# Moving SBUF tiles of a hybrid retention / gated-delta layer: weight buffers at a pitch of 2304 bytes instead of 2176, and everything behind the constants at multiples of 1024 bytes

## The chip, the cores and the metric

The kernel runs on one core of one Trainium2 chip. The metric is device time in microseconds: the median of the timed executions. One further execution was taken with the hardware profiler, and all rows below come from it.

## What is computed

One decoder layer on a float32 stream of 1024 tokens by 2048 columns. A conditioning vector gives shift, scale and gate; the scaled stream goes through one large projection; four retention heads and eight gated-delta heads work on its columns; an output projection, a gated residual and a LayerNorm end it. Cut to its core:

```
mod = silu(c) @ w_ada + b_ada; shift, scale, gate = split(mod, 3)
h = x * (1 + scale) + shift
[rq|rk|rv|rg|gqkv|gg|ga|gb] = h @ w_in              # 2048 x 7184
ret = groupnorm(retention(rotary(rq), rotary(rk), rv)) * silu(rg)
gdn = rmsnorm(gated_delta(l2norm(conv_silu(gqkv)), g(ga), sigmoid(gb))) * silu(gg)
y = concat(ret, gdn) @ w_out                        # 2048 x 2048
out = layernorm(2**0.25 * x + gate * y) * ln_w + ln_b
```

## The kernel before

**Split operands.** Each float32 operand of the two large projections is split into a high part (a cast to the type float32r, on ScalarE) and a low part (the rest, a subtraction, mostly on VectorE), and each product is three matmuls: high with high, high with low, low with high. The stream h stands transposed in SBUF as 16 pairs of tiles `h_hi`, `h_lo` of 128 x 1024 (4096 bytes of each partition). Weights come in units: SyncE's queue loads `w_raw`, L94 casts it to `w_hi`, L95 makes `w_lo`. Each of the three names has two buffers (`wp`, bufs=2), so units use the first and the second buffer in turn, each WU elements long.

**The three places with large matmuls.** `gemm_cm` (L410) makes a tile of 128 columns of the projection, transposed: the weights are stationary (128 x 128), h is the moving operand (512 columns). A unit has four row tiles, so 4 x 3 products x 2 halves = 24 matmuls; a tile has four units. `gemm_v` (L445) has h stationary and 256 weight columns moving, in units of 48 matmuls. The output projection (L1047) has pieces of the mixed heads (`ms`) stationary and 512 columns of the output weights (`wr`) moving; both live in row tiles of 4096 bytes.

**Order.** TensorE's order is written by hand: the projections call `tick()` after each matmul, and the heads' own steps are placed in between. The other engines' order, and that of SyncE's DMA queue, comes out of a scheduler that ranks instructions by what they wait for, a buffer's reuse included. TensorE's program starts with the conditioning (VectorE accumulates 16 row groups of `w_ada` into `acc`, L194), goes on with retention head 0, eight gated-delta heads, retention heads 1 to 3, and the output projection. The last gated-delta head's recurrence runs while `gemm_v` of retention head 1 is multiplied: per chunk VectorE makes `w` (L872) and the state `gs` (L887) from matmuls, and the next matmuls wait for them.

**Gate columns.** `gate_unit` (L372 to L392) loads 256 KB of `w_ada` into `graw` (one of the two buffers of the tag `gb`) and adds it to `gacc` on VectorE; 64 such units are called from the projections of retention heads 1 to 3, 16 of them in those of head 1. `gacc` and the second copy of the rotary table `rot` (1 MB, L482) stand in the pool `rp`, which is allocated on the right of SBUF when head 1 has its `gemm_v` behind it and the gated-delta pool `gp` on the left is given up.

**Where tiles stand.** Pools on the left grow up from byte 0 of each partition, those on the right down from the end. At 0 lies the descriptor scratch of the DMAs that GpSimd issues (16384 bytes by default), then the constants, then the tiles `h` and `ms`, then `w_raw`, `w_hi`, `w_lo` (later `raw`, `wr`), then the pools of the heads. In the program as built the `h` tiles start at 20960 and then every 4096 bytes; the two `w_hi` buffers at 156384 and 158560, the two `w_lo` buffers at 160736 and 162912; `gp` reaches up to 175824, and `rp`'s table is placed at 165600. A buffer of 544 elements is 2176 bytes, 8.5 times 256. So measured from a multiple of 256 bytes, all `h` tiles, `ms` and `wr` and the first buffers of `w_hi` and `w_lo` start 224 bytes behind it, the second buffers of both 96 bytes behind it. Steps inside a buffer are multiples of 512 bytes in `gemm_cm` and leave this as it is.

Of the kernel before, what the change touches and what calls it, by code (L numbers as in the profile page):

```python
# [7 lines left out]
F32 = mybir.dt.float32  # L8
# [7 lines left out]
P = 128  # L16
T = 1024
# [41 lines left out]
def hybrid_layer_kernel(ctx: ExitStack, tc: tile.TileContext, x, c, w_ada, b_ada, w_in, gdn_conv_w,  # L59
                        gdn_a_log, gdn_dt_bias, ret_gn_w, ret_gn_b, gdn_norm_w, w_out, ln_w, ln_b,  # L60
                        tab, out):
    nc = tc.nc
    V, S, G, PE = nc.vector, nc.scalar, nc.gpsimd, nc.tensor

    ctx.enter_context(tc.manual_schedule(engines={mybir.EngineType.PE}))
    const = ctx.enter_context(tc.tile_pool(name="const", bufs=1, side="left"))
# [15 lines left out]
    def load_const(name):  # L82
        lo, hi = TAB[name]
        t = const.tile([P, hi - lo], F32, name=name, tag=name)
        nc.sync.dma_start(out=t, in_=tab[:, lo:hi])
        return t

    WU = 544

    def split(raw, n, eng_l=None):  # L90
        hi = wp.tile([P, WU], F32R, name="w_hi", tag="w_hi")
# [26 lines left out]
            V.tensor_tensor(out=w, in0=w, in1=y, op=ALU.mult)  # L118
            V.scalar_tensor_tensor(out=y, in0=w, scalar=1.5, in1=y, op0=ALU.add, op1=ALU.mult)

# [1 line left out]
    ident = load_const("ident")  # L122
    cs = const.tile([P, KT], F32, name="cs")
    nc.sync.dma_start(out=cs, in_=c[0].rearrange("(p r) -> p r", r=KT))
    ones = const.tile([P, 1], F32, name="ones")
# [7 lines left out]
    cw = const.tile([P, 96], F32, name="cw")  # L133
    gnp = const.tile([P, 32], F32, name="gnp")

# [1 line left out]
    # The projections' sums over the first NA row tiles of g1, GDN k0 and v (two token tiles) wait in SBUF.  # L137
    NA = 5
    RATE = 1.7
    pa_ctx = ctx.enter_context(ExitStack())  # L140
# [4 lines left out]
    with ExitStack() as st:  # L145
# [75 lines left out]
                PE.transpose(ph[:, j * P:(j + 1) * P], xss[kt][:, 4 * i + j], ident)  # L221
            S.copy(xTs[kt][:, i * 512:(i + 1) * 512], ph)

        # The last item is the first unit of the next tile's weights.
        items = [(0, kt) for kt in range(NA)] + [(1, kt) for kt in range(KT)] + [(2, NA)]
        ps0 = []

# [105 lines left out]
    xid = load_const("xid")  # L333
    colsc, kdec, qdec = load_const("colsc"), load_const("kdec"), load_const("qdec")

    # Steps of the heads' own work wait here; the projections call tick() after each matmul, so that
    # each step is placed among matmuls that do not depend on it.
    # The heads' own sequence keeps its order; output steps (aux) come first when they are due.
    clock = [0.0]
    heads, aux, ao = [], [], [1]  # L340

# [24 lines left out]
    def small_ps():  # L366
        return ps.tile([P, 512], F32, name="ps", tag="ps")

# [1 line left out]
    gate_state = dict(i=0, acc=None)  # L370

    def gate_unit():  # L372
# [18 lines left out]
            V.tensor_tensor(out=row, in0=pgt[0:1, :], in1=row, op=ALU.add)  # L391
            nc.sync.dma_start(out=gate_d[:, cb * 512:(cb + 1) * 512], in_=row)  # L392

# [1 line left out]
    def gemm_cm(col, gate=False, part=None):  # L395
        pt = pg.tile([P, T], F32, name="pg", tag="pg")
        k0 = 0 if part is None else NA
# [77 lines left out]
                                       op0=ALU.add, op1=ALU.mult)  # L475
        return sg

# [1 line left out]
    def load_rot(pool, tag="rot"):  # L479
        lo, _ = TAB["rot"]  # L480
        t = pool.tile([P, 2, T], F32, name="rot", tag=tag)
# [115 lines left out]
            store(out=mixed[kti][:, tsl], in_=mx)  # L597
            yield 0

# [1 line left out]
    def conv_silu(pt, ti):  # L601
        y = mp.tile([P, T], F32, name="yc", tag="y", bufs=3)
        S.activation(out=y, in_=pt, func=AF.Copy, scale=cw[:, 72 + ti:73 + ti])  # L603
# [95 lines left out]
    def gdn_keys(h, st, k, dec, Pm):  # L699
        sup = mp.tile([P, 2048], F32, name="sup", tag="x8")  # L700
        A = sup[:, 0:1024].rearrange("p (j i) -> p j i", i=32)
        nb = c4(sup[:, 1024:2048])
        kt_ = mp.tile(B8, F32, name="ktok", tag="ktok")
        ss = gp.tile([P, NC], F32, name="ssk", tag="ssk")
        ets = []
        for hf in range(2):
            gb = gate_rows(h, hf)
            decay_matrix(h, hf, gb, gb, dec)
            ets.append(c4(gb))
        for hf in range(2):  # L710
            pk = small_ps()
            for j in range(4):
                ch = 4 * hf + j
                PE.transpose(pk[:, j * P:(j + 1) * P], k[:, ch * P:(ch + 1) * P], ident)
            sum_squares(pk, ss[:, 4 * hf:4 * hf + 4])
            V.tensor_tensor(out=kt_[:, 4 * hf:4 * hf + 4], in0=c4(pk),
                            in1=dec["ktl"][:, 4 * hf:4 * hf + 4, h:h + 1].broadcast_to(B4), op=ALU.mult)
            yield 4
        rk = gp.tile([P, NC], F32, name="rk", tag="rk")
        sk = gp.tile([P, NC], F32, name="sk", tag="sk")  # L720
        co = gp.tile([P, NC], F32, name="co", tag="co")
        nco = gp.tile([P, NC], F32, name="nco", tag="nco")
        V.tensor_scalar(out=ss, in0=ss, scalar1=1e-6, scalar2=None, op0=ALU.add)
        rsqrt(gp, rk, ss, NC, "k")
        V.tensor_tensor(out=sk, in0=ss, in1=rk, op=ALU.mult)
        V.tensor_tensor(out=rk, in0=rk, in1=rk, op=ALU.mult)
        V.tensor_tensor(out=co, in0=rk, in1=dec["beta"][:, :, h], op=ALU.mult)
        V.tensor_scalar(out=nco, in0=co, scalar1=-1.0, scalar2=None, op0=ALU.mult)
        for hf in range(2):
            pkk = small_ps()  # L730
            for j in range(4):
                cl = slice((4 * hf + j) * P, (4 * hf + j + 1) * P)
                PE.matmul(pkk[:, j * P:(j + 1) * P], k[:, cl], k[:, cl], start=True, stop=True)  # L733
            for j in range(4):
                ch = 4 * hf + j
                V.scalar_tensor_tensor(out=nb[:, ch], in0=pkk[:, j * P:(j + 1) * P], scalar=nco[:, ch:ch + 1],
                                       in1=ets[hf][:, j], op0=ALU.mult, op1=ALU.mult)
            yield 2
        # 32x32 diagonal blocks of the inverse: each partition has one block and eight of its rows
        s1 = drs.tile([4, NC, 1024], F32, name="s1", tag="s1")  # L740
        for b in range(4):
            bs = slice(32 * b, 32 * b + 32)
            nc.sync.dma_start(out=s1[b].rearrange("c (j i) -> j c i", i=32), in_=nb[bs, :, bs])
        for b in range(4):
            nc.sync.dma_start(out=A[32 * b:32 * b + 32].rearrange("p j i -> p (j i)"),
                              in_=s1[b][None].broadcast_to([4, NC, 1024]))
        X_ = gp.tile([P, 288], F32, name="X", tag="X")
        G.memset(X_, 0.0)
        G.tensor_copy(X_.rearrange("p (m i) -> p m i", i=36)[:, :, 0:4], xid[:, None, :].broadcast_to([P, 8, 4]))
        X = X_[:, :256].rearrange("p (m i) -> p m i", i=32)  # L750
        tmp = gp.tile([P, 8, 32], F32, name="xt", tag="xt")
        for j in range(31):
            cnt = j // 4 + 1
            if cnt <= 2:
                for m in range(cnt):
                    V.scalar_tensor_tensor(out=X[:, m, j + 1:], in0=A[:, j, j + 1:], scalar=X[:, m, j:j + 1],
                                           in1=X[:, m, j + 1:], op0=ALU.mult, op1=ALU.add)
            else:
                sh = [P, cnt, 31 - j]
                V.tensor_tensor(out=tmp[:, :cnt, j + 1:], in0=X[:, :cnt, j:j + 1].broadcast_to(sh),  # L760
                                in1=A[:, j:j + 1, j + 1:].broadcast_to(sh), op=ALU.mult)
                V.tensor_tensor(out=X[:, :cnt, j + 1:], in0=X[:, :cnt, j + 1:], in1=tmp[:, :cnt, j + 1:], op=ALU.add)
        s2 = drs.tile([4, 8, 4, NC, 32], F32, name="s2", tag="s2")
        for b in range(4):
            nc.sync.dma_start(out=s2[b].rearrange("m g c i -> (g c) m i"), in_=X[32 * b:32 * b + 32])
        for b in range(4):
            bs = slice(32 * b, 32 * b + 32)
            nc.sync.dma_start(out=Pm[bs, :, bs], in_=s2[b].rearrange("m g c i -> (m g) c i"))
        st.update(kt=kt_, nb=nb, sk=sk, co=co, due=clock[0] + BASE_WAIT)
# [149 lines left out]
        store(out=mixed[8 + h][:, hs], in_=mx)  # L919
        yield 0  # L920

# [1 line left out]
    gab = const.tile([P, NC, 16], F32, name="gab")  # L923
    with tc.high_priority():
        q_, k_ = (mp.tile([P, T], F32, name="qk0", tag=tag) for tag in ("ktok", "et"))
# [19 lines left out]
    for h in range(GH):  # L945
# [3 lines left out]
        v = conv_silu(gemm_cm(GV + h * P), 16 + h)  # L949
# [21 lines left out]
            if r < RH - 1 or e == 0:  # L971
                gate_ready(sgs, pt)
    ph1.close()
# [1 line left out]
    wp = ctx.enter_context(tc.tile_pool(name="wp2", bufs=1, side="left", reuse_waits="tile"))  # L975

    rings = dict(raw=0, wr=0)

    def ring(tag, n, m):
        """The first n of n + m tiles take the space that is free first."""  # L980
        i = rings[tag]
        rings[tag] = i + 1
        return dict(tag=tag, bufs=n) if i % (n + m) < n else dict(tag=tag + "_", bufs=m)

    def split_tile(src, own=False, urgent=True):
        """A row tile's high part and, beside it, the rest."""
        raw = wp.tile([P, 512], F32, name="raw", **ring("raw", 4, 2))
        with ExitStack() if own else tc.high_priority():
            nc.sync.dma_start(out=raw, in_=src)
        t = hp.tile([P, T], F32R, name="ms", tag="h") if own else wp.tile([P, T], F32R, name="wr", **ring("wr", 3, 1))  # L990
        with tc.high_priority() if urgent else ExitStack():
            S.copy(t[:, :512], raw)  # L992
        with tc.high_priority() if urgent else ExitStack():
            V.tensor_tensor(out=t[:, 512:], in0=raw, in1=t[:, :512].bitcast(F32), op=ALU.subtract)  # L994
        return t
# [27 lines left out]
    for hf in range(2):  # L1023
# [4 lines left out]
        for cb in range(4):  # L1028
# [92 lines left out]
            if not last:  # L1121
                rows = []
# [68 lines left out]
```

## Time and profile before

| what | us |
|---|---|
| timed executions (three) | 1993.68, 1992.58, 1999.07; median 1993.68 |
| span of the profiled execution | 2000.5, which is 6.8 over that median |
| TensorE busy in it | 1884.4 (94%) |
| VectorE, ScalarE, GpSimd busy | 1173.2, 552.2, 245.8 |
| TensorE's chain lines L410, L1047, L445 | 44%, 13%, 6% of the span |

A row of the page's groups reads: line, engine, operation, output<-inputs, shapes, count, then busy time, mean duration of one, and idle time of the engine just before. Matmuls overlap, so their pace is the distance from start to start, not the mean duration. Windows give busy time per engine in a stretch; PEclk is the share of TensorE's full clock that was granted.

### The profile page before, as it was taken

How to read it: one execution, taken by the hardware profiler on the slowest of the kernel's cores; microseconds unless marked ns; L12 is line 12 of the kernel's file. 1: busy time of each engine (PE TensorE's matmuls, PEld its weight loads, DVE VectorE, ACT ScalarE, POOL GpSimd, SP SyncE). 2: the span in 40 equal slices, each digit the busy share in tenths (PEclk: the TensorE clock that was granted, in tenths of full speed). 3: DMA queues.
4: the chain of work that ended last, by engine and by line, in shares of the span. 5: the costliest groups of instructions: out<-in, count | busy, mean ns of one | idle time of the engine just before them, and what ended most of it. 6: DMA issues, size and time to landing. Idle time of an engine off the chain costs nothing.

```text
span 2000.5 us, 27960 instructions
## 1 busy us (share of the span) xinstructions
PE 1884.4 (94%) x10272; PEld 1580.9 (79%) x10272; DVE 1173.2 (59%) x2943; ACT 552.2 (28%) x1241; POOL 245.8 (12%) x203
## 2 busy tenths in 40 slices
PE   3788999999999999999999999999999999998996
PEld 3566887787878888787878898898898878886885
DVE  7987346656675757475575744544542534459557
ACT  2433223232323232322323231211211232234221
POOL 3544001000000010000000010010010010005102
PEclk9899999999999999999999999999999999999998
DMA  9995322222221222222221224144141157345532
GB/s 269 277 282 151 83 65 71 59 67 59 66 57 46 72 52 72 48 69 56 70 57 46 72 80 126 43 143 132 41 134 48 44 187 249 110 145 173 191 108 96
DMA packets 293387, 210.76 MB, mean 105 GB/s; under 512 B 44969, under 2 KB 253050, under 8 KB 292482
## 3 DMA queue, kind: packets, MB, share of 16 engines
q1 hardware_dynamic: 290626, 200.59, 36.3%
q0 software_dynamic: 2624, 8.39, 1.2%
q8 instruction: 80, 1.31, 0.3%
q14 instruction: 57, 0.47, 0.1%
HBM read 190.01 MB, written 18.92 MB: 104 GB/s over the span
## 4 chain that ended last, share of the span: by engine, by line
PE 71%; DMA 5%; DVE 4%; issue 1%; ACT 1%; POOL 1%; SPq 0%; ACTq 0%; DVEq 0%; POOLq 0%
PE pg L410 44%; PE po L1047 13%; PE pg L445 6%; DMA gb<-gc_d 3%; DMA raw<-mixed 2%; DVE et L695 1%; PE ps L892 1%; PE ps L876 1%; PE ps L870 1%; PE ps L733 1%; PE ps L891 1%; PE ps L882 1%; PE ps L543 1%; DMA graw<-in_w_ada_dram 0%; DVE z L1102 0%
## 5 line engine op out<-in xcount | busy, mean ns | idle before, releaser
L410 PE MATMUL pg<-h_hi,w_hi 128*128 128x512 f32 x1420 | 470.2, 403 | 0.1
L410 PE MATMUL pg<-h_hi,w_lo 128*128 128x512 f32 x1420 | 466.2, 402 | 2.1 <-DVE w_lo L95 2.1
L410 PE MATMUL pg<-h_lo,w_hi 128*128 128x512 f32 x1420 | 465.0, 401 | 0.0
L94 ACT CAST w_hi<-w_raw 128x512 fp32r<-128x512 f32 (+3 forms) x239 | 146.5, 613 | 679.2 <-PE pg L410 481.9
L1047 PE MATMUL po<-wr,ms 128*128 128x512 f32 x1380 | 319.4, 392 | 11.2 <-DVE wr L994 7.9
L1047 PEld LDWEIGHTS po<-wr,ms 128*128 128x128 f32 x1380 | 259.3, 189 | 69.5 <-DVE wr L994 10.7
L410 PEld LDWEIGHTS pg<-h_hi,w_lo 128*128 128x128 f32 x1420 | 265.5, 189 | 55.4 <-DVE w_lo L95 3.3
L410 PEld LDWEIGHTS pg<-h_lo,w_hi 128*128 128x128 f32 x1420 | 266.5, 189 | 52.7
L410 PEld LDWEIGHTS pg<-h_hi,w_hi 128*128 128x128 f32 x1420 | 265.4, 189 | 53.7 <-ACT w_hi L94 1.7
L95 DVE TENSOR_TENSOR w_lo<-w_raw,w_hi 128x512 fp32r<-128x512 f32 (+2 forms) x217 | 153.9, 710 | 218.5 <-ACT w_hi L94 213.3
L994 DVE TENSOR_TENSOR wr<-raw,wr 128x512 fp32r<-128x512 f32 x116 | 88.0, 763 | 108.6 <-ACT wr L992 108.6
L445 PE MATMUL pg<-w_lo,h_hi 128*128 128x256 f32 (+1 forms) x502 | 143.4, 286 | 2.1 <-DVE w_lo L95 2.1
L445 PE MATMUL pg<-w_hi,h_hi 128*128 128x256 f32 (+1 forms) x502 | 143.5, 286 | 0.1
L445 PE MATMUL pg<-w_hi,h_lo 128*128 128x256 f32 (+1 forms) x502 | 143.3, 286 | 0.0
L992 ACT CAST wr<-raw 128x512 fp32r<-128x512 f32 x116 | 71.4, 621 | 155.6 <-PE po L1047 145.9
L194 DVE SCALAR_TENSOR_TENSOR acc<-wa,cs,acc 128x256 f32<-128x256 f32 x224 | 111.8, 564 | 4.0 <-DMA wa<-in_w_ada_dram 3.2
L445 PEld LDWEIGHTS pg<-w_lo,h_hi 128*128 128x128 f32 x502 | 95.1, 190 | 3.1 <-DVE w_lo L95 3.0
L445 PEld LDWEIGHTS pg<-w_hi,h_hi 128*128 128x128 f32 x502 | 95.2, 190 | 2.2 <-ACT w_hi L94 1.7
L445 PEld LDWEIGHTS pg<-w_hi,h_lo 128*128 128x128 f32 x502 | 95.1, 190 | 0.0
L606 DVE SCALAR_TENSOR_TENSOR yc<-pg,cw,yc 128x1023 f32<-128x1023 f32 (+2 forms) x69 | 88.2, 1279 | 2.9 <-ACT yc L603 2.0
L385 DVE SCALAR_TENSOR_TENSOR gacc<-graw,cs,gacc 128x512 f32<-128x512 f32 x60 | 48.4, 807 | 55.7 <-DMA graw<-in_w_ada_dram 55.3
L212 POOL TENSOR_TENSOR h_lo<-xT,h_hi 128x1024 fp32r<-128x1024 f32 x16 | 52.0, 3252 | 85.9 <-ACT h_hi L211 85.9
(243 smaller groups left out, 2235.7 us busy)
## 6 DMA issues: line engine op xcount, KB each, us to landing
w_raw<-in_w_in_dram SPq DMA_DIRECT2D x216, 256.0 KB
wa<-in_w_ada_dram SPq DMA_DIRECT2D x128, 256.0 KB
raw<-in_w_out_dram SPq DMA_DIRECT2D x128, 256.0 KB
graw<-in_w_ada_dram SPq DMA_DIRECT2D x64, 256.0 KB
xs<-in_x_dram SPq DMA_DIRECT2D x16, 512.0 KB
gb<-gc_d SPq DMA_DIRECT2D x32, 256.0 KB
raw<-mixed SPq DMA_DIRECT2D x32, 256.0 KB
z<-in_x_dram SPq DMA_DIRECT2D x32, 256.0 KB
```

What stands on the lines that cost most here:

```text
L94: S.copy(hi[:, :n], raw[:, :n])
L95: (eng_l or V).tensor_tensor(out=lo[:, :n], in0=raw[:, :n], in1=hi[:, :n].bitcast(F32), op=ALU.subtract)
L194: V.scalar_tensor_tensor(out=a, in0=wr, scalar=cs[:, r:r + 1], in1=a, op0=ALU.mult, op1=ALU.add)
L212: G.tensor_tensor(out=h_lo, in0=xT, in1=h_hi.bitcast(F32), op=ALU.subtract)
L385: V.scalar_tensor_tensor(out=a, in0=raw[:, :512], scalar=cs[:, r:r + 1], in1=a, op0=ALU.mult, op1=ALU.add)
L410: PE.matmul(pt[:, i * 512:(i + 1) * 512], w[:, kk], hh[:, i * 512:(i + 1) * 512], start=(kt == k0 and w is hi and hh is hH[kt]), stop=(kt ...
L445: PE.matmul(dst(tt), hh[:, tsl], w[:, kk], start=(kt == k0 and first_in_bank and hh is hH[kt] and w is hi), stop=(kt == KT - 1 and hh is h ...
L543: PE.matmul(po[:, :DV], sc[:, ch], vt[:, ch], start=(ch == 0), stop=True)
L606: V.scalar_tensor_tensor(out=y[:, s:], in0=pt[:, :T - s], scalar=cw[:, j * 24 + ti:j * 24 + ti + 1], in1=y[:, s:], op0=ALU.mult, op1=ALU.add)
L992: S.copy(t[:, :512], raw)
L994: V.tensor_tensor(out=t[:, 512:], in0=raw, in1=t[:, :512].bitcast(F32), op=ALU.subtract)
L1047: PE.matmul(pts[tt], m[:, a + tt * P:a + (tt + 1) * P], w, start=(n == 0 and a == 0 and w is wh), stop=(n == KT - 1 and a == 512))
```

## The change

Three numbers of placement: WU grows from 544 to 576 elements, so that a buffer is 2304 bytes, 9 times 256; a constant tile `pad` of 136 elements is put behind `ident`, with one column of it written; and the descriptor scratch is made 4096 bytes. No instruction's shape changes.

```diff
-    WU = 544
+    WU = 576
...
     ident = load_const("ident")
+    pad = const.tile([P, 136], F32, name="pad")
+    V.memset(pad[:, 0:1], 0.0)
     cs = const.tile([P, KT], F32, name="cs")
...
-    nc = _bacc.Bacc("TRN2", target_bir_lowering=False, num_devices=1)
+    nc = _bacc.Bacc("TRN2", target_bir_lowering=False, num_devices=1,
+                    dynamic_dma_scratch_size=4096)
```

Comments are dropped as well, and two lines come in ahead of the rest, so that a line of the kernel before stands two lines lower after. In the changed program the `h` tiles start at 9216 and then every 4096 bytes; the `w_hi` buffers at 144896 and 147200, the `w_lo` buffers at 149504 and 151808, all at multiples of 256; `raw`, `wr`, `ms` at multiples of 1024. The pools on the right, among them all tiles into which the conditioning and the inputs are loaded, stand where they stood. The left side is about 11 KB shorter: `gp` ends at 164848, below the table of `rp` at 165600.

So `rp` no longer shares bytes with `gp`, and the scheduler orders its tiles anew. TensorE's, ScalarE's and GpSimd's order is the same; SyncE's and VectorE's differ at these places. In SyncE's queue, at the start of the heads (before):

```order
L625 DMA alog<-in_gdn_a_log_dram 128x8
L482 DMA rot<-in_tab_dram 128x2048
L103 DMA w_raw<-in_w_in_dram 128x3x128
L626 DMA dtb<-in_gdn_dt_bias_dram 128x8
L103 DMA w_raw<-in_w_in_dram 128x4x128 x2
L103 DMA w_raw<-in_w_in_dram 128x3x128
```

and in the changed program:

```order
L627 DMA alog<-in_gdn_a_log_dram 128x8
L484 DMA rot<-in_tab_dram 128x2048
L103 DMA w_raw<-in_w_in_dram 128x3x128
L628 DMA dtb<-in_gdn_dt_bias_dram 128x8
L484 DMA rot<-in_tab_dram 128x2048
L103 DMA w_raw<-in_w_in_dram 128x4x128 x2
```

The second table load has moved here, some 1000 us ahead of its first use. In the same queue, in retention head 1 (the rows 2x256 are units of `gemm_v`, 4x128 those of `gemm_cm`), before:

```order
L678 DMA gb<-gc_d 128x4x128
L379 DMA graw<-in_w_ada_dram 128x512
L103 DMA w_raw<-in_w_in_dram 128x2x256
L379 DMA graw<-in_w_ada_dram 128x512
L103 DMA w_raw<-in_w_in_dram 128x2x256 x4
L482 DMA rot<-in_tab_dram 128x2048
L379 DMA graw<-in_w_ada_dram 128x512 x2
L103 DMA w_raw<-in_w_in_dram 128x4x128
L379 DMA graw<-in_w_ada_dram 128x512 x4
L103 DMA w_raw<-in_w_in_dram 128x4x128
```

and in the changed program:

```order
L680 DMA gb<-gc_d 128x4x128
L381 DMA graw<-in_w_ada_dram 128x512
L103 DMA w_raw<-in_w_in_dram 128x2x256
L381 DMA graw<-in_w_ada_dram 128x512 x6
L103 DMA w_raw<-in_w_in_dram 128x2x256
L381 DMA graw<-in_w_ada_dram 128x512 x4
L103 DMA w_raw<-in_w_in_dram 128x2x256
L381 DMA graw<-in_w_ada_dram 128x512 x5
L103 DMA w_raw<-in_w_in_dram 128x2x256
L381 DMA graw<-in_w_ada_dram 128x512 x2
L103 DMA w_raw<-in_w_in_dram 128x2x256
L103 DMA w_raw<-in_w_in_dram 128x4x128 x16
```

Sixteen further gate loads now stand between units of `gemm_v` instead of between those of `gemm_cm`. VectorE's order in the last gated-delta head's recurrence follows this; before:

```order
L885 COPY gs<-ps 128x128
L872 SCALAR_TENSOR_TENSOR w<-ps,neg,vs 128x128
L887 SCALAR_TENSOR_TENSOR gs<-gs,egl,ps 128x128
L872 SCALAR_TENSOR_TENSOR w<-ps,neg,vs 128x128
L95 TENSOR_TENSOR w_lo<-w_raw,w_hi 128x512
L887 SCALAR_TENSOR_TENSOR gs<-gs,egl,ps 128x128
```

and in the changed program:

```order
L384 TENSOR_SCALAR gacc<-graw,cs 128x512
L887 COPY gs<-ps 128x128
L874 SCALAR_TENSOR_TENSOR w<-ps,neg,vs 128x128
L387 SCALAR_TENSOR_TENSOR gacc<-graw,cs,gacc 128x512 x2
L889 SCALAR_TENSOR_TENSOR gs<-gs,egl,ps 128x128
L387 SCALAR_TENSOR_TENSOR gacc<-graw,cs,gacc 128x512
L874 SCALAR_TENSOR_TENSOR w<-ps,neg,vs 128x128
L387 SCALAR_TENSOR_TENSOR gacc<-graw,cs,gacc 128x512
L95 TENSOR_TENSOR w_lo<-w_raw,w_hi 128x512
L889 SCALAR_TENSOR_TENSOR gs<-gs,egl,ps 128x128
```

All 16 sums of the first gate block now stand among the recurrence's steps.

## Rows read from the trace of the kernel before

**Rows 1.** The page's head, and its line of busy times.

```profile
span 2000.5 us, 27960 instructions
PE 1884.4 (94%) x10272; PEld 1580.9 (79%) x10272; DVE 1173.2 (59%) x2943; ACT 552.2 (28%) x1241; POOL 245.8 (12%) x203
```

**Rows 2.** Windows: stretch, length, busy time (instructions) per engine, PEclk, DMA share, GB/s.

```profile
50.00:100.00 50.00, 36.05 (x166) 29.88 (x166) 48.73 (x91) 21.59 (x29) 26.80 (x12) 0.86 1.06 277
166.00:320.00 154.00, 142.19 (x802) 123.37 (x801) 83.78 (x201) 46.40 (x92) 21.77 (x20) 0.99 0.29 75
540.00:650.00 110.00, 107.69 (x626) 88.83 (x625) 69.61 (x217) 32.48 (x97) 7.96 (x9) 1.00 0.23 58
1180.00:1200.00 20.00, 20.00 (x173) 20.00 (x172) 7.30 (x23) 4.57 (x15) 1.61 (x2) 1.00 0.34 118
1200.00:1220.00 20.00, 20.00 (x150) 19.08 (x149) 10.74 (x15) 3.79 (x5) 0.58 (x1) 1.00 0.63 190
1318.00:1337.00 19.00, 18.57 (x156) 18.37 (x156) 10.74 (x14) 4.35 (x8) 3.79 (x4) 1.00 0.55 169
```

**Rows 3.** The page's groups: the large matmuls of the three places.

```profile
L410 PE MATMUL pg<-h_hi,w_hi 128*128 128x512 f32 x1420 | 470.2, 403 | 0.1
L410 PE MATMUL pg<-h_hi,w_lo 128*128 128x512 f32 x1420 | 466.2, 402 | 2.1 <-DVE w_lo L95 2.1
L410 PE MATMUL pg<-h_lo,w_hi 128*128 128x512 f32 x1420 | 465.0, 401 | 0.0
...
L1047 PE MATMUL po<-wr,ms 128*128 128x512 f32 x1380 | 319.4, 392 | 11.2 <-DVE wr L994 7.9
...
L445 PE MATMUL pg<-w_hi,h_hi 128*128 128x256 f32 (+1 forms) x502 | 143.5, 286 | 0.1
```

**Rows 4.** TensorE's timeline, retention head 1: every twelfth row of L410 (start, us, ...).

```profile
1214.98 0.62 PE L410 MATMUL pg<-h_hi,w_hi 128*128 128x512 f32 x2
...
1220.56 0.62 PE L410 MATMUL pg<-h_hi,w_hi 128*128 128x512 f32 x2
...
1226.03 0.64 PE L410 MATMUL pg<-h_hi,w_hi 128*128 128x512 f32 x2
...
1231.62 0.62 PE L410 MATMUL pg<-h_hi,w_hi 128*128 128x512 f32 x2
...
1237.08 0.64 PE L410 MATMUL pg<-h_hi,w_hi 128*128 128x512 f32 x2
```

**Rows 5.** The chain that ended last: start, us, matmuls without a gap.

```profile
869.23 23.05 PE pg L410 x100
...
1200.82 14.32 PE pg L445 x120
1215.14 48.84 PE pg L410 x212
...
1659.99 137.60 PE po L1047 x607
```

**Rows 6.** Timeline of the last gated-delta head's recurrence, TensorE and VectorE.

```profile
1163.76 0.35 DVE L872 SCALAR_TENSOR_TENSOR w<-ps,neg,vs 128x128 f32<-128x128 f32 x1 [0.97 <-PE ps L870]
...
1164.52 0.38 PE L876 MATMUL ps<-w,Pm 128*128 128x128 f32 x2
...
1166.12 0.35 DVE L887 SCALAR_TENSOR_TENSOR gs<-gs,egl,ps 128x128 f32<-128x128 f32 x1 [2.01 <-PE ps L882]
1167.73 0.35 DVE L872 SCALAR_TENSOR_TENSOR w<-ps,neg,vs 128x128 f32<-128x128 f32 x1 [1.27 <-PE ps L870]
```

**Rows 7.** VectorE's gate sums: their tile's group (ns), and its waits (us, times, longest).

```profile
L385 DVE SCALAR_TENSOR_TENSOR gacc<-graw,cs,gacc x60: 746/752/1762, 1195.9 to 1493.7; 128x512 f32<-128x512 f32 x60
...
DVE gacc L385 <- DMA graw<-in_w_ada_dram: 55.3, 46, 3.9
```

**Rows 8.** GpSimd's DMAs: packets, MB, share of 16 engines; median us to landing.

```profile
q0 software_dynamic: 2624, 8.39, 1.2%
...
mixed<-mxr POOLq DMA_DIRECT2D x12, 256.0 KB, 3.3
```

## The prediction

> **What bounds the kernel now.** I read the page's line of busy times first, then windows over the whole span, then TensorE's chain. TensorE is busy for 1884.4 of 2000.5 us [rows 1]. Until about 170 us it waits: in 50 to 100 us it is busy for 36 of 50 us while VectorE has 48.7 and the DMA engines are full [rows 2]. From there on it hardly stops: 107.7 of 110 us in a gated-delta head, 20.00 of 20.00 at 1180 and at 1200 us, at the full clock [rows 2]. So before 170 us TensorE's pace is worth nothing, and behind it nearly every nanosecond of a large matmul is a nanosecond of the kernel. The large matmuls are 3 x 1420 of L410, 1380 of L1047 and 3 x 502 of L445 [rows 3], 7146 together.
>
> **The pace of L410 has two values.** The reader should look at where units begin in a stretch where nothing is interleaved. Twelve rows of two matmuls are one unit of 24. The units take 1220.56 - 1214.98 = 5.58, then 5.47, 5.59 and 5.46 us [rows 4]: long and short in turn. Per matmul that is (5.58 + 5.59) / 48 = 232.7 ns and (5.47 + 5.46) / 48 = 227.7 ns. The two w buffers alternate with the units, and by the program's operand addresses the first and third of these units have their weights in the second buffers, 96 bytes behind a multiple of 256; the second and fourth have the first buffers, 224 bytes behind one, like the h tiles that stream past them. The mean over such stretches is the same elsewhere: 48.84 / 212 = 230.4 ns and, inside a gated-delta head, 23.05 / 100 = 230.5 ns [rows 5]; half of 232.7 and half of 227.7 is 230.2. The output projection, whose both operands stand at 224, runs at 137.60 / 607 = 226.7 ns [rows 5]. So weights that stand at another distance from a multiple of 256 than the moving operand cost about 5 ns, and weights at the same distance do not.
>
> A page speaks against this. The Trainium skill (SBUF — State Buffer, "Who interferes with whom") gives TensorE two independent read ports for the moving and the stationary operand and says that it never waits on anyone; by it a tile's place could not change the pace, and the change would be worth nothing in TensorE. The trace does not agree: 5.58 against 5.47 us for the same 24 matmuls [rows 4].
>
> **The change, part by part.**
>
> *Weights at multiples of 256.* After it both buffers and h have distance 0, so by the reading above all units run at the short pace. Half of 4260 matmuls, 2130, gain 5.0 ns each: 10.6 us. A matmul next to an interleaved step of a head is paced by that step too; I take off a little for these and count -10. From the same rows the least is 0 (something else than the distance alternates), the most is that L410 comes down to the 226.7 ns of the output projection, (230.4 - 226.7) x 4260 = 15.8 us.
>
> *L445 and L1047.* L445 runs at 14.32 / 120 = 119.3 ns for 256 columns [rows 5], a stretch that has both buffers in it; I see no second pace to remove and count 0, with 1 ns either way, 1.5 us, as bounds. L1047 has equal distances already: 0.
>
> *The common distance, 0 instead of 224.* No large matmul of the trace starts at a multiple of 256, so only bounds can be had. Below: 512 columns take 226.7 ns and 256 take 119.3, so a column takes 0.42 ns and each matmul has 226.7 - 214.8 = 11.9 ns on top. If all of that came from starting off a multiple, 7146 x 11.9 = 85 us would go. Above: all of L410 and L1047 at the slow 232.7 ns, which is 2.3 x 4260 + 6.0 x 1380 = 18 us more. The nearest rows are the two with equal distances (L410's short units and L1047, a nanosecond apart), so I take 0.
>
> *Gate sums among the last gated-delta head's recurrence.* 16 sums of 0.75 us [rows 7] now stand before `w` and `gs` on VectorE, and what is queued behind a sum that waits for its load is the recurrence, for which TensorE waits. VectorE is idle there for 1.27 us before `w` and for 2.01 us before `gs` [rows 6], so two sums per chunk of 4 us fit if their data is there. `w` is ready at 1164.11 and is used at 1164.52 [rows 6]: the slack is 0.4 us. A late load costs what exceeds it: in its stretches `gacc` waited for 55.3 / 46 = 1.2 us per load [rows 7]. At best nothing, at worst 16 x 1.2 = 19 us. Where the same sums and loads stand between units of `gemm_v` in head 2, TensorE lost 0.43 us of 19 [rows 2], but no gated-delta recurrence ran there. I take +2, nearer to that row. Where the sums stood before, TensorE was busy for all of 1200 to 1220 us [rows 2], so taking them away there gives nothing.
>
> *The second table load at the start of the heads.* 1 MB in a stretch where the DMA engines are busy for 0.29 [rows 2]; at the 277 GB/s of the full queue it takes 3.8 us, ahead of weight loads. The two weight buffers loaded ahead cover that: 0, and 3.8 us if they do not.
>
> *Scratch of 4 KB, pad.* GpSimd issues 36 stores, 2624 packets in all [rows 8], 73 per store and under 5 per engine, tens of microseconds apart: 0. If the last four waited for the one ahead, 4 x 3.3 = 13 us [rows 8], the bound. `pad` is one memset of one column at the start, where VectorE waits: 0. The tiles of the first 170 us that VectorE and the DMA fill on the right have not moved: 0.
>
> **Sum.** -10 + 2 = -8 us: 1992.5 on the profiled span of 2000.5. That span is 6.8 us over the median of the runs shown, so I put the same difference on the median: 1993.68 - 8 = 1986, with -14 to -2 around it, 1980 to 1992. A difference of under 0.3%, 6 us, is about what a measurement of this kernel cannot tell from no change.
>
> **Rivals.**
>
> *The on-top part shrinks too.* Speaking for it: two placements that differ only by 128 bytes already differ by 5 ns, so a start inside such a stretch may cost in itself. Against it: L410's short units and L1047 end at one value, and no row has a start at 0. A quarter of 11.9 ns is 21 us, half is 43, so with the -8 it gives 1965 to 1943, and at the very least 1901. The Trainium skill (TensorE: Matmul & The Clock Gate, "Wait — 56ns, not 53.3ns?") measures about 2.5 ns on top of a bf16 stream; as an estimate from that page, 9.4 x 7146 = 67 us would go. No run here shows it for this type.
>
> *The place does not matter.* If the alternation belongs to something else that comes with every second unit, or to the ports as the page has it, only the +2 remains: 1996, the same within 0.3%. Against it stand the equal tiles h on both sides of the alternation and the one constant pace of L1047.
>
> *Distance 0 is a bad one.* If what counts is not the equal distance but the place itself, 224 being good and 96 bad, then 0 may be as 96 is. All units of L410 are then at 232.7 ns and L1047 follows: 18 + 2 = 20 us more, 2014. It decides as soon as the common pace of L410 is above 230.4 ns. Nothing in the trace speaks for or against 0 itself.
>
> *The recurrence eats the gain.* With every sum late by its 1.2 us, -10 + 19 = +9, so 2003. It turns the sign from 0.6 us per sum on.
>
> **Chances.** My forecast 52%; the on-top part as well 17%; no effect of the place 17%; 0 a bad place 8%; the recurrence 6%. Of the forecast's share I put three fifths below -6 us: faster by over 0.3% is 0.31 + 0.17 = 0.48. Within 0.3%: 0.21 + 0.14 + 0.02 = 0.37. Slower: 0.03 + 0.08 + 0.04 = 0.15. The range leaves out the lower half of the on-top case and the bad place: 1950 to 2004; the forecast's own is 1980 to 1992.
>
> **What would show it.** Unit starts of L410 in head 1 at equal distances of 5.46 to 5.48 us, and a chain row of about 227.5 ns per matmul, show the first step right; 5.58 and 5.47 in turn show it wrong; all at 5.58 is the bad place. A pace of L1047 clearly under 226.7 ns is the on-top part. Waits of TensorE for `w` and `gs` between 1160 and 1195 us, and of `gacc` for `graw` on VectorE there, show the price of the gate sums; TensorE idle behind 185 us by 3 us more would be the table load. The prediction is wrong if the common distance 0 has a pace of its own, which no row could tell.

## The result

| | before | after |
|---|---|---|
| timed executions, same chip (six each) | 1992.58 to 1999.07 us, median 1996.5 | 1983.53 to 1989.22 us, median 1987.06 |
| ratio of after to before, 95% interval | | 0.9947 [0.9932, 0.9961] |
| span of the profiled execution | 2000.5 us | 1984.3 us |

The change makes the kernel faster by 0.53%, 9.4 us of 1996.5. The two profiled executions lie 16.2 us apart, which is more: each is one execution, executions of one kernel spread over 6 us here, and the profiled one of before is none of its six and longer than all of them. In a later set of executions, in which both kernels took longer, the pair stood at 0.9960 (below).

The profile after, read in the order of the rows of before. A line of the kernel before stands two lower. The page's head, busy times and groups of large matmuls, which answer to [rows 1] and [rows 3]:

```profile
span 1984.3 us, 27946 instructions
PE 1873.7 (94%) x10272; PEld 1578.2 (80%) x10272; DVE 1169.9 (59%) x2944; ACT 552.9 (28%) x1241; POOL 253.1 (13%) x203
...
L412 PE MATMUL pg<-h_hi,w_hi 128*128 128x512 f32 x1420 | 465.6, 400 | 0.0
L412 PE MATMUL pg<-h_hi,w_lo 128*128 128x512 f32 x1420 | 462.8, 399 | 2.3 <-DVE w_lo L95 2.3
...
L1049 PE MATMUL po<-wr,ms 128*128 128x512 f32 x1380 | 319.0, 392 | 9.9 <-DVE wr L996 8.0
...
L447 PE MATMUL pg<-w_hi,h_hi 128*128 128x256 f32 (+1 forms) x502 | 143.8, 286 | 0.1
```

The busy time of each of the two L412 groups shown is down by 3.4 to 4.6 us; the output projection and `gemm_v` have the busy time that they had. TensorE's timeline in retention head 1, where nothing is interleaved; every fourth row of `h_hi,w_hi` is shown, a unit has four, one per row tile, so that a step is a unit of 24 matmuls, as in [rows 4]:

```profile
1204.21 0.63 PE L412 MATMUL pg<-h_hi,w_hi 128*128 128x512 f32 x2
...
1209.67 0.62 PE L412 MATMUL pg<-h_hi,w_hi 128*128 128x512 f32 x2
...
1215.11 0.62 PE L412 MATMUL pg<-h_hi,w_hi 128*128 128x512 f32 x2
...
1220.55 0.62 PE L412 MATMUL pg<-h_hi,w_hi 128*128 128x512 f32 x2
...
1225.99 0.62 PE L412 MATMUL pg<-h_hi,w_hi 128*128 128x512 f32 x2
```

The units take 5.46, 5.44, 5.44 and 5.44 us. The alternation of 5.58 and 5.47 [rows 4] is gone, and the units are a little shorter than the short ones were. The chain that ended last (start, us, what ran without a gap) says the same of whole stretches, and answers to [rows 5]:

```profile
636.49 22.70 PE pg L412 x100
...
1082.04 22.70 PE pg L412 x100
...
1189.98 14.39 PE pg L447 x120
1204.37 48.08 PE pg L412 x212
...
1639.88 141.54 PE po L1049 x623
```

L412 runs at 48.08 / 212 = 226.8 ns (before 230.4), L447 at 14.39 / 120 = 119.9 (119.3), the output projection at 141.54 / 623 = 227.2. The row of before that answers to the last one is

```profile
1656.03 141.56 PE po L1047 x623
```

so 227.2 as well; the 607 matmuls of [rows 5] are a part of it. So the whole gain in pace is L412's.

What the change costs shows in the last gated-delta head. The timeline of TensorE and VectorE there (in brackets the idle time before, and what ended it), against [rows 6]:

```profile
1151.15 0.38 PE L884 MATMUL ps<-u,ktok 128*128 128x128 f32 x2
...
1151.57 1.54 DVE L387 SCALAR_TENSOR_TENSOR gacc<-graw,cs,gacc 128x512 f32<-128x512 f32 x2 [2.00 <-DMA graw<-in_w_ada_dram]
...
1153.02 0.34 DVE L889 SCALAR_TENSOR_TENSOR gs<-gs,egl,ps 128x128 f32<-128x128 f32 x1
...
1153.42 0.49 PE L872 MATMUL ps<-gs,yc 128*128 128x128 f32 x2 [0.49 <-DVE gs L889]
1155.06 0.75 DVE L387 SCALAR_TENSOR_TENSOR gacc<-graw,cs,gacc 128x512 f32<-128x512 f32 x1 [1.70 <-DMA graw<-in_w_ada_dram]
1155.73 0.34 DVE L874 SCALAR_TENSOR_TENSOR w<-ps,neg,vs 128x128 f32<-128x128 f32 x1
...
1156.13 0.49 PE L878 MATMUL ps<-w,Pm 128*128 128x128 f32 x2 [1.27 <-DVE w L874]
```

VectorE stands at a gate sum for 2.00 us because `graw` has not landed. `gs` is queued behind it; its input, the product of L884, has been begun at 1151.15, but it runs only at 1153.02, and TensorE waits. At 1155.06 the same happens to `w`. TensorE's two longest waits of that stretch, 1082 to 1190 us (us in total, times, longest):

```profile
PE ps L878 <- DVE w L874: 1.5, 2, 1.3
PE ps L884 <- ACT u L880: 1.1, 1, 1.1
```

The early second table load left no mark. A window, columns as in [rows 2]:

```profile
166.00:320.00 154.00, 142.77 (x802) 124.00 (x801) 81.77 (x202) 44.33 (x90) 24.71 (x22) 0.98 0.29 76
```

TensorE is busy for 142.77 of the 154 us in which the table arrives, against 142.19 before.

### The profile page after: what moved, and what is told of

It is laid out like the page before. It is cut to its first block, busy times and chain, and to the rows that moved or that the text cites. A ratio compares the mean times of both kernels' runs of the same rounds, so it can differ in the third digit from the quotient of the medians.

```text
span 1984.3 us, 27946 instructions
## 1 busy us (share of the span) xinstructions
PE 1873.7 (94%) x10272; PEld 1578.2 (80%) x10272; DVE 1169.9 (59%) x2944; ACT 552.9 (28%) x1241; POOL 253.1 (13%) x203
## 4 chain that ended last, share of the span: by engine, by line
PE 69%; DMA 6%; DVE 6%; issue 1%; ACT 1%; POOL 0%; SPq 0%; DVEq 0%; ACTq 0%; POOLq 0%
PE pg L412 42%; PE po L1049 13%; PE pg L447 6%; DMA gb<-gc_d 3%; DMA graw<-in_w_ada_dram 1%; DMA raw<-mixed 1%; DVE z L1104 1%; PE ps L735 1%; PE ps L878 1%; DVE wr L996 1%; PE ps L872 1%; PE ps L545 1%; PE ps L893 1%; PE ps L894 1%; POOL yc L859 0%
## 5 line engine op out<-in xcount | busy, mean ns | idle before, releaser
L412 PE MATMUL pg<-h_hi,w_hi 128*128 128x512 f32 x1420 | 465.6, 400 | 0.0
L412 PE MATMUL pg<-h_hi,w_lo 128*128 128x512 f32 x1420 | 462.8, 399 | 2.3 <-DVE w_lo L95 2.3
L412 PE MATMUL pg<-h_lo,w_hi 128*128 128x512 f32 x1420 | 461.2, 399 | 0.0
L412 PEld LDWEIGHTS pg<-h_hi,w_lo 128*128 128x128 f32 x1420 | 264.7, 189 | 52.5 <-DVE w_lo L95 3.5
L412 PEld LDWEIGHTS pg<-h_hi,w_hi 128*128 128x128 f32 x1420 | 264.8, 189 | 51.3 <-ACT w_hi L94 1.7
L412 PEld LDWEIGHTS pg<-h_lo,w_hi 128*128 128x128 f32 x1420 | 265.7, 189 | 49.4
L447 PE MATMUL pg<-w_lo,h_hi 128*128 128x256 f32 (+1 forms) x502 | 143.4, 286 | 1.7 <-DVE w_lo L95 1.7
L447 PE MATMUL pg<-w_hi,h_hi 128*128 128x256 f32 (+1 forms) x502 | 143.8, 286 | 0.1
L447 PE MATMUL pg<-w_hi,h_lo 128*128 128x256 f32 (+1 forms) x502 | 143.3, 286 | 0.0
L447 PEld LDWEIGHTS pg<-w_lo,h_hi 128*128 128x128 f32 x502 | 95.6, 190 | 2.5 <-DVE w_lo L95 2.4
L447 PEld LDWEIGHTS pg<-w_hi,h_hi 128*128 128x128 f32 x502 | 95.6, 190 | 2.2 <-ACT w_hi L94 1.7
L447 PEld LDWEIGHTS pg<-w_hi,h_lo 128*128 128x128 f32 x502 | 95.6, 190 | 0.0
L214 POOL TENSOR_TENSOR h_lo<-xT,h_hi 128x1024 fp32r<-128x1024 f32 x16 | 58.0, 3624 | 80.8 <-ACT h_hi L213 80.8
```

The lines of the kernel that those rows point to most:

```text
L214: G.tensor_tensor(out=h_lo, in0=xT, in1=h_hi.bitcast(F32), op=ALU.subtract)
L412: PE.matmul(pt[:, i * 512:(i + 1) * 512], w[:, kk], hh[:, i * 512:(i + 1) * 512], start=(kt == k0 and w is hi and hh is hH[kt]), stop=(kt ...
L447: PE.matmul(dst(tt), hh[:, tsl], w[:, kk], start=(kt == k0 and first_in_bank and hh is hH[kt] and w is hi), stop=(kt == KT - 1 and hh is h ...
```

## The experiments

"Distance" below is the start of the weights minus the start of h, modulo 256 bytes, by the programs' operand addresses. The kernel before has units at 0 and units at 128 in turn; the changed one has all at 0. Its two buffers lie 2304 bytes apart, 9 times 256, and its units have one pace, so that a step of 256 bytes itself does not count.

**The pitch alone.** The kernel before with the new pitch and a scratch that is 1024 bytes shorter, which makes room for the wider buffers. h and all weights stand 224 bytes behind a multiple of 256; the order of every engine is that of before.

```diff
-    WU = 544
+    WU = 576
...
+                    dynamic_dma_scratch_size=15360)
```

> Pitch of 2304 bytes alone, everything else as before (the scratch is 1024 bytes smaller to make room, so that all tiles keep their 224 bytes behind a multiple of 256, and all engines keep the order of the kernel before). If the equal distance of weights and h is what counts: all units of L410 in head 1 take 5.45 to 5.48 us, the gate sums stay out of the recurrence, and the time is 11 to 13 us under before, ratio 0.994, some 2 to 3 us under the changed kernel. If multiples of 256 or 1024 themselves are what counts: nothing stands on one, units still 5.58 and 5.47 in turn or all 5.58, ratio 0.999 to 1.005.

Measured: ratio 0.9962 [0.9948, 0.9975], a smaller gain than expected. The chain:

```profile
643.24 22.69 PE pg L410 x100
...
1195.41 14.39 PE pg L445 x120
1209.81 48.08 PE pg L410 x212
```

The same 48.08 us for 212 matmuls, with h at 224: the gain needs the equal distance, and a multiple of 256 is not needed.

**The placement alone.** The changed kernel with the old pitch: h at 0, units at distances 0 and 128 in turn, the new order of loads and sums.

```diff
-    WU = 576
+    WU = 544
```

> The changed kernel with the pitch put back to 2176 bytes: h at multiples of 1024, the first w buffers 0 and the second 128 bytes behind a multiple of 256, scratch 4096, the new order of gate sums and table. Equal distance: units 5.58 and 5.47 in turn as before, and the 2 to 3 us of the gate sums in the recurrence on top: ratio 1.000 to 1.002. If h on multiples of 1024 brings the gain: units all 5.47, ratio 0.994 to 0.996.

Measured: ratio 1.0000 [0.9989, 1.0011]. The chain:

```profile
642.33 23.00 PE pg L412 x100
...
1090.74 23.00 PE pg L412 x100
...
1199.81 14.32 PE pg L447 x120
1214.13 48.85 PE pg L412 x212
```

All lengths are those of before to 0.05 us. New scratch, pad and places give nothing without the pitch.

**Everything at 96.** If 96 were a bad place in itself, this would show it.

```diff
-    pad = const.tile([P, 136], F32, name="pad")
+    pad = const.tile([P, 160], F32, name="pad")
```

> The changed kernel with a pad of 160 elements in place of 136: h, ms, wr and all w buffers stand 96 bytes behind a multiple of 256. Equal distance: as the changed kernel, units of 5.45 to 5.48 us, output projection 226.7 ns per matmul, ratio to before 0.994 to 0.996. If 96 is a bad place by itself: all units 5.58, the output projection 232 ns, 18 to 20 us more than the changed kernel, ratio 1.004 to 1.006.

Measured: ratio 0.9969 [0.9958, 0.9980], and again 48.08 us for the 212 matmuls; the pace is as expected, the gain a little smaller. With 224, 0 and 96 giving one pace, a place that is good or bad in itself is ruled out for these three.

**All units 128 apart.** The changed kernel with 128 bytes ahead of the weight buffers, and nothing else.

```diff
+    gap = wp.tile([P, 32], F32, name="gap", tag="gap", bufs=1)
+    V.memset(gap[:, 0:1], 0.0)
```

> The changed kernel with a tile of 128 bytes ahead of the w buffers: h at 0, all w buffers 128 bytes behind a multiple of 256, the output projection's tiles at 0. Equal distance: all units of L410 take 5.58 to 5.60 us, which is 2 x 10.6 = 21 us over the changed kernel, ratio to before 1.005 to 1.008; output projection at 226.7 ns. If the second buffer rather than the distance is slow: units as in the changed kernel or in turn, ratio 0.994 to 1.001.

Measured: ratio 1.0028 [1.0017, 1.0039]. Lines stand two lower than in the changed kernel; the chain:

```profile
1205.23 14.24 PE pg L449 x120
1219.48 49.26 PE pg L414 x212
```

49.26 / 212 = 232.4 ns, the slow pace, now in all units. That settles that the distance makes the pace. The Trainium skill (SBUF — State Buffer, "Who interferes with whom") says that TensorE never waits on anyone. The trace shows 49.26 against 48.08 us for the same matmuls, so the place of these operands does change their pace; whether it is a wait at a port, no run shows. The loss in time is smaller than the pace lets one expect: between this run and the one at 96, on one chip, lie 1.0028 - 0.9969 = 0.59%, 11.8 us, where 4260 matmuls at 232.4 - 226.8 = 5.6 ns would be 23.9.

**The changed kernel again, and with the old order.** In one further set the changed kernel was run once more, and beside it with a scratch of 14336 bytes: the left side is then so long that `rp` shares bytes with `gp` again, and SyncE's and VectorE's order is that of before, with all distances still 0.

```diff
-                    dynamic_dma_scratch_size=4096)
+                    dynamic_dma_scratch_size=14336)
```

> The changed kernel itself once more, beside the next kernel on one chip. Ratio to before as it was, 0.993 to 0.996; if the first measurement was lucky by the chip, 0.996 to 0.998 as the two kernels with equal distances at 224 and at 96.

> The changed kernel with a scratch of 14336 bytes: all tiles at the same distances (0) as in the changed kernel, but the table's place overlaps the gated-delta pool again, so that SyncE's and VectorE's order is that of the kernel before. If the gate sums in the recurrence cost 2 to 3 us: that much faster than the changed kernel, and no waits for w beyond those before between 1150 and 1195 us. If the early table and gate loads are what brought the changed kernel a part of its gain: slower than the changed kernel by 1 to 4 us.

Measured: 0.9960 [0.9944, 0.9976] for the changed kernel, 0.9947 [0.9933, 0.9962] with the old order. The intervals overlap, so the times do not part the two. The traces do, at one place. The changed kernel again:

```profile
639.48 22.70 PE pg L412 x100
...
1086.85 22.70 PE pg L412 x100
...
1196.55 14.39 PE pg L447 x120
1210.93 48.08 PE pg L412 x212
```

and with the old order:

```profile
640.34 22.70 PE pg L412 x100
...
1087.70 22.70 PE pg L412 x100
...
1191.73 14.39 PE pg L447 x120
1206.12 48.08 PE pg L412 x212
```

From the row at 1087 to the L447 row, the stretch with the last recurrence, the changed kernel takes 1196.55 - 1086.85 = 109.70 us, with the old order 1191.73 - 1087.70 = 104.03. In that stretch TensorE waited for `u` and `w` for 2.4 + 1.9 us with the new order, and for `u` alone, 0.9 us, with the old one. Not all of the difference is the order's: the wait for `u` and the clock, below, have a part in it.

**Other pitches.** Two pitches that leave the four buffers at four distances.

```diff
-    WU = 576
+    WU = 584
```

> The changed kernel with a pitch of 2336 bytes: w_hi stands 64 bytes (first buffer) and 96 bytes (second) from h, w_lo 128 and 160 bytes. Nothing was measured between 0 and 128. If the loss is a step, units take 5.46 to 5.60 us with the rows of single products at one of two values; if it grows with the distance up to 128, 64 and 96 lie between 227.9 and 232.4 ns per matmul.

```diff
-    WU = 576
+    WU = 592
```

> The changed kernel with a pitch of 2368 bytes: w_hi stands 128 bytes (first buffer) and 192 bytes (second) from h, w_lo 0 and 64 bytes. By the equal distance the first buffer's w_lo matmuls run at 227.9 ns and its w_hi matmuls at 232.4; 192 and 64 are open, as in the kernel with the pitch of 2336.

Measured: single executions, 2008.21 and 2002.30 us, where before took 2001.66 in the median; 49.27 and 49.19 us for the 212 matmuls of head 1, which is 232.4 and 232.0 ns. In the second, `w_lo` of every other unit stands at distance 0, and the matmuls with `w_lo` take 230 to 231 ns from start to start in either buffer, not 227.9.

**Only `w_lo` apart.** 128 bytes between the `w_hi` and the `w_lo` buffers: 16 matmuls of each unit at distance 0, 8 at 128.

```diff
+    made = []
...
+        if not made:
+            made.append(wp.tile([P, 32], F32, name="gap", tag="gap", bufs=1))
+            V.memset(made[0][:, 0:1], 0.0)
         lo = wp.tile([P, WU], F32R, name="w_lo", tag="w_lo")
```

> The changed kernel with a gap tile between w_hi and w_lo: in every unit w_hi stands at h's distance (0) and w_lo 128 bytes away from it. Equal distance counted pair by pair: 16 matmuls of a unit at 227.9 ns and the 8 with w_lo at 232.4 make 5.51 us per unit of 24. The whole unit must stand at h's distance: about 5.58 us, as with all at 128. Only w_hi counts: 5.47 us.

Measured: 2002.65 us in one execution, before beside it 2000.03. The chain (lines four lower than in the changed kernel):

```profile
1202.98 14.14 PE pg L451 x120
1217.12 49.29 PE pg L416 x212
```

49.29 / 212 x 24 = 5.58 us per unit, as with all at 128. So the price is not one that each matmul pays for its own pair of operands: with a third of the matmuls apart the whole unit is slow. By their starts in that stretch the 16 with `w_hi` take 231 to 232 ns and the 8 with `w_lo` 234.

**All at 64, all at 192.** The gap tile of the run at 128, made 64 and 192 bytes.

```diff
+    gap = wp.tile([P, 16], F32, name="gap", tag="gap", bufs=1)
+    V.memset(gap[:, 0:1], 0.0)
```

> The changed kernel with every weight buffer 64 bytes away from h (modulo 256). A step (equal or not equal): 232.4 ns from matmul to matmul in L412's units, 5.58 us per unit, as with 128. A loss that grows with the distance: about 230.1 ns, 5.52 us. Only multiples of 128 matter: 227.9 ns or a value of its own. The output projection stays at 227 ns in all cases.

```diff
+    gap = wp.tile([P, 48], F32, name="gap", tag="gap", bufs=1)
+    V.memset(gap[:, 0:1], 0.0)
```

> The changed kernel with every weight buffer 192 bytes away from h (modulo 256). A step: 232.4 ns, 5.58 us per unit. A loss by the shorter way round 256 (64 bytes): as the run with 64. A loss that grows with the distance: above 232.4, about 234.6 ns, 5.63 us per unit. The output projection stays at 227 ns.

Measured: one execution each, 2011.79 and 1993.66 us, before 2000.03. The chain at 64:

```profile
1209.96 14.14 PE pg L449 x120
1224.10 49.47 PE pg L414 x212
```

and at 192:

```profile
1198.91 13.62 PE pg L449 x120
1212.53 48.53 PE pg L414 x212
```

No one expectation holds for both: a step comes near at 64 (233.3 against 232.4) and fails at 192. L412's pace is 226.8 ns at 0, 233.3 at 64, 232.4 at 128 and 48.53 / 212 = 228.9 at 192: neither a step nor growing with the distance, nor the same both ways round. And `gemm_v`, in which h is stationary and the weights move, has its own order: 119.9 ns at 0, 118.7 at 128, 117.8 at 64, and 13.62 / 120 = 113.5 at 192. That made up for L412's loss there.

**`gemm_v` shifted.** From that, a kernel meant to beat the others: the old order, L412 at 0, and the 256-column units of `gemm_v` written 192 bytes into their buffers.

```diff
-    def split(raw, n, eng_l=None):
+    def split(raw, n, eng_l=None, o=0):
...
-            S.copy(hi[:, :n], raw[:, :n])
+            S.copy(hi[:, o:o + n], raw[:, :n])
...
-        hi, lo = split(raw, a * n)
+        hi, lo = split(raw, a * n, None, 48 if a == 2 and extra is None else 0)
```

> The kernel of the run with a scratch of 14336 bytes, in which the units of gemm_v that are 256 columns wide are written 192 bytes into their buffers, so that L447's weights stand 192 bytes behind h while L412's stay at h's distance. If the pace of the run with all weights at 192 belongs to the place: 256-column matmuls from 122.0 to 116.5 ns, some 1130 of them back to back, 6 us less than that run, so a ratio of about 0.992. If the place of L412's units around them made it: no change from that run, 0.995.

Measured: ratio 0.9934 [0.9916, 0.9953]. It is the lowest ratio of the study, but its interval holds both values expected, 0.992 and 0.995. The chain:

```profile
639.31 22.70 PE pg L412 x100
...
1086.89 22.70 PE pg L412 x100
...
1192.99 13.62 PE pg L447 x120
1206.60 48.07 PE pg L412 x212
```

The pace of 113.5 ns belongs to the place, with L412's units untouched. Of the 6 us that it promised the profiled spans show 2.1, 1985.1 against 1987.2 with the old order alone; the next part looks for the rest.

**Where each kernel's time goes.** The rows of the chain cut each profiled span at the same instructions: the first and the fifth stretch of 100 matmuls in the gated-delta heads, and the L447 stretch of 120. For the kernel before these are

```profile
642.98 23.00 PE pg L410 x100
...
1094.69 23.05 PE pg L410 x100
```

and the L445 row of [rows 5], so 642.98, then 1094.69 - 642.98 = 451.71, then 1200.82 - 1094.69 = 106.13, then 2000.5 - 1200.82 = 799.7. In the same way, with TensorE's granted clock of the middle two stretches in brackets (1.00 is 2.4 GHz, 0.50 would be 1.2 GHz):

| kernel | distance | to the 1st x100 | to the 5th x100 | recurrence, to x120 | to the end |
|---|---|---|---|---|---|
| before | 0, 128 | 642.98 | 451.71 (0.99) | 106.13 (1.00) | 799.7 |
| placement alone | 0, 128 | 642.33 | 448.41 (1.00) | 109.07 (0.98) | 799.7 |
| after | 0 | 636.49 | 445.55 (1.00) | 107.94 (1.00) | 794.3 |
| after, again | 0 | 639.48 | 447.37 (0.99) | 109.70 (0.98) | 795.4 |
| all at 96 | 0 | 639.54 | 447.28 (0.99) | 108.69 (0.98) | 796.2 |
| pitch alone | 0 | 643.24 | 447.90 (0.99) | 104.27 (1.00) | 796.1 |
| old order | 0 | 640.34 | 447.36 (0.99) | 104.03 (1.00) | 795.5 |
| `gemm_v` shifted | 0 | 639.31 | 447.58 (0.99) | 106.10 (0.98) | 792.1 |
| all at 192 | 192 | 643.25 | 449.04 (1.00) | 106.62 (1.00) | 793.0 |
| all at 128 | 128 | 643.59 | 452.16 (1.00) | 109.48 (1.00) | 798.6 |
| all at 64 | 64 | 646.99 | 453.44 (1.00) | 109.53 (0.98) | 800.0 |

Each is one execution. The first column varies by 6.8 us among kernels of one pace (636.49 to 643.24); it holds the stretch in which DMA and VectorE set the time, and the 16.2 us between the first two profiles have 6.5 of it. The last column varies by 2 us at one pace (794.3 to 796.2), and it is 3.5 to 5.4 below that of the two kernels with alternating distances.

Two things in the middle columns are not the placement's. One is the clock: before and the placement alone have one pace and one distance, and their second stretches differ by 3.3 us, 451.71 at 0.99 against 448.41 at 1.00; in before, windows at 710.5:713.9 and 1048.4:1051.8 read 0.50. The other is TensorE's wait for `u` early in the recurrence. It has two sizes, 0.9 to 1.1 us (after, pitch alone, old order, all at 192, all at 128) and 2.2 to 2.4 us (the other six). In the six VectorE's `et`, some 6 us ahead, takes 2.15 to 2.21 us in place of 1.14, and GpSimd's `yc` starts 0.57 to 0.80 us behind the start of `et`; in the five it starts 0.84 to 1.03 us behind. Behind the longer wait the granted clock falls to half, in all of the six but before. A row of the timeline and a window show it, with the old order

```profile
1152.76 0.49 PE L884 MATMUL ps<-u,ktok 128*128 128x128 f32 x2 [0.91 <-ACT u L880]
...
1153.66:1157.07 3.41, 3.41 (x32) 3.41 (x31) 0.45 (x3) 0.90 (x6) 0.00 (x0) 1.00 0.20 73
```

and with `gemm_v` shifted, whose order is the same:

```profile
1153.27 0.49 PE L884 MATMUL ps<-u,ktok 128*128 128x128 f32 x2 [2.26 <-ACT u L880]
...
1153.66:1157.07 3.41, 3.41 (x19) 3.41 (x19) 0.91 (x3) 1.01 (x7) 0.00 (x0) 0.52 0.35 118
```

In the same 3.41 us 19 matmuls start in place of 32. A wait that is 1.35 us longer and a clock that costs about 1.6 us (an estimate, 0.48 of 3.41) move this stretch by some 3 us. Either order and several distances stand in both groups, so what is compared there must be of one group.

## Why the prediction held, and what was mis-sized

*Weights at multiples of 256, -10.* The mechanism is right: the distance is the cause (128 apart by a gap tile alone: 49.26 against 48.08 us), and the pitch alone brings 0.38%, 7.6 us, with an interval of 5.0 to 10.4. Two errors in the term worked against each other. Per matmul in an uninterrupted stretch the gain is 230.4 - 226.8 = 3.6 ns, not half of 5.0, since the short units became shorter too, down to the output projection's pace: the case that I had as the upper bound, 15.8 us. But only part of it arrives. Between the first and the fifth x100 row lie 1537 matmuls of L412, most of them among steps of the heads. At one granted clock the alternation costs 451.71 - 447.37 = 4.3 us there (0.99; before against the changed kernel again) or 448.41 - 445.55 = 2.9 us (1.00; the placement alone against the changed kernel): 2.8 or 1.9 ns per matmul of 3.6, each from two executions. Over the whole kernel the timed sets show half: 7.6 of 3.6 x 4260 = 15.3 us for the pitch alone, 11.8 of 23.9 between all at 96 and all at 128. Taking off "a little" for the interleaved matmuls was too little. Where the other half goes is not shown; the heads' steps between the matmuls and the granted clock are candidates.

*L445 and L1047, 0.* Right: 119.3 to 119.9 ns, and 141.56 to 141.54 us for the same 623 matmuls. That `gemm_v` had a pace of 113.5 to be had could not be read from a trace with two distances.

*The common distance, 0.* Right; h at 224, 96 and 0 give 48.08 us alike.

*Gate sums in the recurrence, +2.* The mechanism is right and the size too small. Among the kernels with the short wait for `u` and the full clock, the changed one takes 107.94 us in the stretch, the two with the old order at the new pace 104.27 and 104.03: 3.8 us, from one execution against two. At the old pace it is 109.07 - 106.13 = 2.9 us, of which the fallen clock of the first explains about 1.6. I took the value near a row of a place where no recurrence ran. The timed pairs (0.9960 against 0.9947) bound it no better than to a few microseconds either way.

*Table load, scratch, pad, 0.* TensorE's share in the window of the table load did not fall. The scratch was tested only together with the order: 4096 and 14336 bytes end alike, 794.3 to 796.2 us and 795.5 in the last column.

*The sum, -8.* Timed: -9.4 us in the first set, and in the later one 0.40% of 2001.66, -8.0. The forecast of 1986 us is met by 1987.06. Part of this is luck in the base: I put the difference on a median of three, 1993.68, and six executions have 1996.5. Part is luck in the terms: the pitch alone was timed at -7.6, and with 3.8 for the order the sum would be -4; the timed sets, whose intervals are some 3 us wide either way, do not resolve the terms.

*The rivals.* "The place does not matter" falls by the run at 128. "Distance 0 is a bad one" and "the on-top part shrinks too" fall together: the pace of the output projection is 227.2 ns at 0 and at 224, so nothing of the 11.9 ns on top goes away by the place. "The recurrence eats the gain" is there at up to 3.8 us of the 19 that it had as its worst, less than the gain.

*Where the shift of `gemm_v` went.* 14.39 - 13.62 = 0.77 us per 120 matmuls is in the rows. The last column is 3.4 us lower than with the old order alone (792.1 against 795.5), but the stretch with the recurrence is 2.1 us longer (106.10 against 104.03). The longer wait for `u` and the fallen clock, some 3 us together, are enough for that. Kernels without the shift have the same wait and the same fall, so it is not shown that the shift brings them.

*Open.* What in the chip makes the distance count is not known. The runs exclude a price per matmul (only `w_lo` apart slows the whole unit) and, among distances of 0, 64, 128 and 192, every rule with distance as a step, or growing with it; they give no rule in its place. Nor is it known why units at distance 0 between units at 128 take 227.7 ns per matmul and not 226.8.

## What to carry to other kernels

Where TensorE streams float32r operands without a gap, look at the start of both operands modulo 256 bytes: here a buffer pitch of 8.5 times 256 gave every second unit another pace, which shows as unit starts that alternate. Of a difference in pace read in an uninterrupted stretch and taken times all matmuls, about half arrived here. A change of layout alone can reorder loads: look at what stops or starts sharing bytes, and try giving the freed space back where the old order was better. Before a stretch of one profile is set against that of another, look at the granted clock in both: here it moved a stretch of 450 us by 3.3 us at one and the same pace.

## What the runs showed that was not expected

- 512 float32r columns against 128 x 128 weights take 226.8 ns with all weights at distance 0, 228.9 at 192, 232.4 at 128 and 233.3 at 64; with 256 moving columns the best of the four is another one, 113.5 ns with the moving weights 192 bytes behind h and 119.9 at equal distance.
- A unit in which only the `w_lo` buffers stand 128 bytes apart, 8 of its 24 matmuls, takes 5.58 us like one in which all do.
- The size of the descriptor scratch, 4096 or 14336 bytes, changes the order of DMA loads, by whether two pools share bytes: 107.94 against 104.03 us in the last recurrence at one granted clock. The size and the order were never changed apart.
- In all 14 profiles a wait of TensorE for `u` of 0.9 to 1.1 or of 2.2 to 2.4 us goes with a VectorE row of 1.14 or of 2.15 to 2.21 us ahead of it, and in six of the eight with the longer wait the granted clock falls to half behind it. This moves the last recurrence by up to some 3 us, whatever the placement.
